# First mixer: multiplying four heads by a column each with four ScalarE activations instead of one VectorE instruction

## The chip, the cores and the metric

The kernel runs on one core of a Trainium2 chip. The metric is the device time of one execution in microseconds (us). The engines are called as in the profile: PE (TensorE: matmuls and transposes), PEld (its weight loads), DVE (VectorE), ACT (ScalarE), POOL (GpSimd) and SP (SyncE, which issues the large transfers).

## What is computed

The reference is a two-layer trunk over 256 positions of width 2048. Each layer is a modulated norm, a mixer, a gated residual, a second modulated norm, an MLP and a gated residual. The first layer's mixer runs eight gated DeltaNet heads and eight banded attention heads of 128 channels each beside one another. The parts that the change touches are the per-position factors in it:

```python
q = l2_norm(q.reshape(b_, t_, GDN_HEADS, GDN_DK)) * (GDN_DK ** -0.5)
k = l2_norm(k.reshape(b_, t_, GDN_HEADS, GDN_DK))
...
u = jnp.einsum('bhnij,bhnje->bhnie', tmat, vc * bc[..., None])
q_dec = qc * jnp.exp(gcum)[..., None]
...
o = rms_norm(o, norm_w) * jax.nn.silu(z.reshape(b_, t_, GDN_HEADS, GDN_DV).astype(f32))
...
qh = rms_norm(heads(q), q_norm_w).astype(f32) * (ATT_DH ** -0.5)
kh = rms_norm(heads(k), k_norm_w).astype(f32)
```

In each of these a matrix of 128 positions (the partitions) by 128 channels of one head is multiplied by one number per position.

## The kernel before

The weights stream from memory in pieces of 1 MB (`raw`). ACT casts each to a high part `wh` (L317), DVE takes the difference as a low part `wl` (L321), and PE multiplies both (L308); these products are in most of the program what PE does. Beside them the modulation vectors are reduced on DVE from pieces of the same size (`mraw`, L439, 2048 columns each), which share four buffers with the weight pieces, so SP can send the next transfer only when DVE has released a buffer.

The first mixer lies between about 240 and 560 us. It works in two groups of four heads (group 0 and group 1), and in tiles of 128 positions by four heads (128x512). The DeltaNet part prepares each tile in `gdn_tile`: squares of k and q (L1042, on ACT), an inverse square root by three Newton steps of tiny DVE instructions (L263 to L277), decay factors `gu` (L1046) and `gE`, then `gV` (v times a factor of k, L1069), then an inverse in six levels (L1100 to L1123: matmul, DVE mask into `gY`, matmul, DVE subtraction into `gX`, transposes, ACT copy into `gXt`). `gdn_group` then runs the chain over the tiles: `gvn` (L1147), the state `gS`, `gR` (L1160), `gqS` (L1165), the second `gvn` (L1171), the outputs `go` with their squares (L1185), an inverse root (`goy`), the multiplication of `go` (L1197), and transposes into a unit that the output projection reads. For the attention heads `att_qk` copies q or k out of PSUM (L1240), squares them (L1244), makes an inverse root (`ay`, L1247 and L271 to L276), multiplies (`aq`, L1250) and transposes (L1255 to L1257). It is called four times: q and k of group 0 near 250 us, q of group 1 near 363 us, k of group 1 near 427 us.

All of it is written as generators, whose steps are interleaved with the steps of the weight products. Each instruction has a priority from the order of emission, with the reductions of L439 put 20 later, and a list scheduler with a model of the durations sets the order on each engine. PE fills the time in these chains with products that are already loaded: `pg` from `wh` and `wl` in pieces of 512 columns, later of 256.

Of the kernel before, what the change touches and what calls it, by code (L numbers as in the profile page):

```python
# [13 lines left out]
AF = mybir.ActivationFunctionType  # L14
ALU = mybir.AluOpType
# [51 lines left out]
def wait(*tasks):  # L67
    for t in tasks:
        while not t.done:
            yield False  # L70
# [42 lines left out]
class Trunk:  # L113
# [212 lines left out]
    def split(self, src, hi, lo):  # L326
        for _ in self.split_steps(src, hi, lo):
            pass

    def bc(self, col, n=P):  # L330

        return col.unsqueeze(2).to_broadcast([P, col.shape[1], n])
# [691 lines left out]
    def gdn_tile(self, hg, t, kf, qf, vf, G):  # L1024
# [3 lines left out]
        nc = self.nc  # L1028
# [3 lines left out]
        for n, src in ((0, kf), (1, qf)):  # L1032
            ps = self.pm()
# [17 lines left out]
        nk = self.small(4, "gnk")  # L1051
        nc.vector.tensor_tensor(nk, v[:, :4], rn[:, :4], op=ALU.mult)
        be = self.small(4, "gbe")
# [5 lines left out]
        ps = self.pm()  # L1059
# [5 lines left out]
        ps = self.pm()  # L1065
        for h in range(4):
            self.tr(ps[:, h], vf[:, h, T])
        V = self.s2(tag="gV")
        nc.vector.tensor_tensor(V, ps, self.bc(nk), op=ALU.mult)  # L1069
        G["V", t] = V  # L1070
        yield

        ps = self.pm()
# [10 lines left out]
        ps = self.pm()  # L1084
# [6 lines left out]
        ps = self.pm()  # L1091
# [8 lines left out]
        for s in (2, 4, 8, 16, 32, 64):  # L1100
            nb = P // (2 * s)
            part = lambda a, n: a.rearrange("p h (b n c) -> p h b n c", n=2, c=s)[:, :, :, n]
            ps = self.pm()
# [6 lines left out]
            ps = self.pm()  # L1110
            if s < 64:
# [4 lines left out]
                ps = self.pm()  # L1116
# [10 lines left out]
    def gdn_group(self, hg, kc, qc, vc, gates):  # L1127

        nc = self.nc
        yield from wait(kc, qc, vc, gates)  # L1130
        yield
        kf, qf, vf = kc.result, qc.result, vc.result
        G = {}
        tiles = [Task(self.gdn_tile(hg, t, kf, qf, vf, G)) for t in range(2)]
        while not all(t.done for t in tiles):
            for t in tiles:
                if not t.done:
                    t.step()
            if all("X" + str(n) in G for n in range(2)):
                self.prep[hg].done = True  # L1140
            yield

        ps = self.pm()
        for h in range(4):
            self.mm(ps[:, h], G["Xt", 0][:, h], G["V", 0][:, h])
        v0 = self.s2(tag="gvn")
        nc.vector.tensor_tensor(v0, ps, self.bc(G["be", 0]), op=ALU.mult)  # L1147
        yield
        ps = self.pm()
        for h in range(4):  # L1150
            self.mm(ps[:, h], G["kd"][:, h], v0[:, h])
        S = self.s2(tag="gS")
        nc.scalar.copy(S, ps)
        yield
        ps = self.pm()
        for h in range(4):
            self.mm(ps[:, h], kf[:, h, P:], S[:, h])
        R = self.s2(tag="gR")
        for h in range(4):
            nc.vector.scalar_tensor_tensor(R[:, h], ps[:, h], self.neg_eg[:, hg * 4 + h : hg * 4 + h + 1], G["V", 1][:, h], op0=ALU.mult, op1=ALU.add)  # L1160
        qs = self.pm()
        for h in range(4):
            self.mm(qs[:, h], qf[:, h, P:], S[:, h])
        qS = self.s2(tag="gqS")
        nc.vector.tensor_tensor(qS, qs, self.bc(self.eg[:, hg * 4 : hg * 4 + 4]), op=ALU.mult)  # L1165
        yield
        ps = self.pm()
        for h in range(4):
            self.mm(ps[:, h], G["Xt", 1][:, h], R[:, h])
        v1 = self.s2(tag="gvn")  # L1170
        nc.vector.tensor_tensor(v1, ps, self.bc(G["be", 1]), op=ALU.mult)  # L1171
        ss = self.small(8, "goss")
        outs = []
        for t in range(2):
            yield
            ps = self.pm()
            for h in range(4):
                self.mm(ps[:, h], G["Pt", t][:, h], (v0, v1)[t][:, h])
            o = self.s2(tag="go")
            if t == 0:  # L1180
                nc.scalar.copy(o, ps)
            else:
                nc.vector.tensor_tensor(o, qS, ps, op=ALU.add)
            for h in range(4):
                nc.scalar.activation(ps[:, h], o[:, h], AF.Square, accum_out=ss[:, t * 4 + h : t * 4 + h + 1])  # L1185
            outs.append(o)
        yield
        r = self.small(8, "gor")
        for t in range(2):
            nc.vector.tensor_copy(r[:, t * 4 : t * 4 + 4], G["rq", t])  # L1190
        nc.vector.tensor_tensor(ss, ss, r, op=ALU.mult)
        nc.vector.tensor_tensor(ss, ss, r, op=ALU.mult)
        nc.vector.tensor_scalar(ss, ss, 1.0 / P, EPS, op0=ALU.mult, op1=ALU.add)
        rr = self.rsqrt(ss, 8, "go")
        nc.vector.tensor_tensor(rr, rr, r, op=ALU.mult)
        for t in range(2):
            nc.vector.tensor_tensor(outs[t], outs[t], self.bc(rr[:, t * 4 : t * 4 + 4]), op=ALU.mult)  # L1197
        yield

        res = qf  # L1200
        for t in range(2):
            ps = self.pm()
            for h in range(4):
                self.tr(ps[:, h], outs[t][:, h])
            nc.scalar.copy(res[:, :, t * P : t * P + P], ps)
            yield
        return res
# [24 lines left out]
    def att_qk(self, ps, nw, part=None):  # L1232

        nc = self.nc
        a, v = [], self.small(8, "ass")
        for t in range(2):
            x = self.s2(tag="aq")
            flat = x.rearrange("p h d -> p (h d)")
            if part is None:
                nc.scalar.copy(flat, ps[t])  # L1240
            else:
                nc.vector.tensor_tensor(flat, ps[t], part[:, t], op=ALU.add)
            for h in range(4):
                nc.scalar.activation(ps[t][:, h * P : h * P + P], x[:, h], AF.Square, accum_out=v[:, t * 4 + h : t * 4 + h + 1])  # L1244
            a.append(x)
            yield
        nc.vector.tensor_scalar(v, v, 1.0 / P, EPS, op0=ALU.mult, op1=ALU.add)  # L1247
        r = self.rsqrt(v, 8, "a")
        for t in range(2):
            nc.vector.tensor_tensor(a[t], a[t], self.bc(r[:, t * 4 : t * 4 + 4]), op=ALU.mult)  # L1250
        yield
        res = self.unit()
        for t in range(2):
            pt = self.pm()
            for h in range(4):  # L1255
                self.tr(pt[:, h], a[t][:, h])
            nc.scalar.activation(res[:, :, t * P : t * P + P], pt, AF.Copy, scale=nw)  # L1257
            if t == 0:
                yield
        return res  # L1260
# [551 lines left out]
```

## Time and profile before

| | |
|---|---|
| time, median of three runs | 2714.98 us (2714.04 to 2716.82) |
| time of the profiled execution | 2719.37 us |
| its span | 2717.6 us |
| mean granted clock of TensorE | 0.998 |
| PE, DVE, ACT busy | 2665.0, 2147.6, 1351.2 us |
| DVE, ACT busy in 240–260 us | 14.09, 17.59 of 20 |
| DVE, ACT busy in 340–360 us | 19.63, 14.34 of 20 |

A busy share is the mean over the whole span, and stages differ; so the stage of the mixer is read in windows. The chain of waits goes back from the last instruction to what released each; where PE carries it, PE never stood still. The rows that were read stand below.

### The profile page before, as it was taken

The page shows a single profiled execution, that of the slowest core. Times are in us where ns is not written, and L with a number is a line of the kernel's source. Part 1 is how long each engine was busy: PE and PEld are TensorE (multiplying, and loading weights), DVE is VectorE, ACT ScalarE, POOL GpSimd, SP SyncE. Part 2 cuts the span into 40 slices and gives each one's busy share as a digit, 9 for nine tenths or more (in the row PEclk, how much of TensorE's full clock was granted, in tenths as well). Part 3 has the DMA queues.
Part 4 walks back from the last instruction along what each step waited for, and adds up shares of the span by engine and source line. Part 5 has one row for each costly group of instructions (what it writes and reads, how often), then busy time and mean ns, then how long its engine had stood idle before and what let it go on. Part 6 is the DMA issues. An engine that isn't in the chain of part 4 may idle for free.

```text
span 2717.6 us, 39677 instructions
## 1 busy us (share of the span) xinstructions
PE 2665.0 (98%) x15664; PEld 2350.4 (86%) x15664; DVE 2147.6 (79%) x3081; ACT 1351.2 (50%) x1976; POOL 24.5 (1%) x98
## 2 busy tenths in 40 slices
PE   5999999999999999999999999999999999999999
PEld 5887989888888888888888888888888888888888
DVE  7998998987888888889889876897777855555554
ACT  3444454546445354454556544665555354454452
POOL 1000000000000000000000000000000000000000
PEclk9999999999999999999999999999999999999999
DMA  9986487867899898988456665554558855555554
GB/s 341 353 325 235 172 301 272 294 241 282 322 339 328 328 336 330 333 331 307 165 185 217 217 234 200 203 185 172 196 177 293 324 201 188 188 191 193 186 192 134
DMA packets 100459, 680.06 MB, mean 250 GB/s; under 512 B 11185, under 2 KB 14513, under 8 KB 19377
## 3 DMA queue, kind: packets, MB, share of 16 engines
q1 hardware_dynamic: 95376, 669.07, 68.5%
q10 hardware_dynamic: 4896, 8.46, 1.0%
q8 instruction: 123, 2.02, 0.3%
q14 instruction: 64, 0.52, 0.1%
HBM read 675.33 MB, written 2.16 MB: 249 GB/s over the span
## 4 chain that ended last, share of the span: by engine, by line
PE 90%; DVE 6%; DMA 1%; ACT 1%; issue 1%; SPq 0%; ACTq 0%; DVEq 0%
PE pw L308 70%; PE pg L308 13%; PE pm L311 4%; PE pm L308 3%; DVE mraw L439 2%; DVE wl L321 1%; PE pm L314 1%; DMA mraw<-in_mod_dram 1%; DVE u L1592 0%; ACT wh L317 0%; DVE hf L862 0%; ACT pm L1042 0%; DMA raw<-in_w_ab_dram 0%; DMA x<-in_x_dram 0%; DVE u L865 0%
## 5 line engine op out<-in xcount | busy, mean ns | idle before, releaser
L317 ACT CAST wh<-raw 128x1024 fp32r<-128x1024 f32 x870 | 907.1, 1051 | 1031.6 <-PE pw L308 732.9
L321 DVE TENSOR_TENSOR wl<-raw,wh 128x1024 fp32r<-128x1024 f32 x870 | 1048.7, 1220 | 463.8 <-ACT wh L317 349.6
L308 PE MATMUL pw<-u,wh 128*128 128x512 f32 x5584 | 1321.6, 391 | 2.6 <-DVE pad L973 1.9
L308 PEld LDWEIGHTS pw<-u,wh 128*128 128x128 f32 x5584 | 1032.2, 188 | 208.2 <-issue 3.3
L308 PEld LDWEIGHTS pw<-u,wl 128*128 128x128 f32 x5584 | 702.3, 191 | 21.3 <-issue 2.1
L308 PE MATMUL pw<-u,wl 128*128 128x256 f32 x5584 | 714.5, 283 | 0.3 <-DVE wl L321 0.3
L439 DVE SCALAR_TENSOR_TENSOR mraw<-mraw,crow 128x2048 f32<-128x2048 f32 x192 | 438.0, 2283 | 17.8 <-DMA mraw<-in_mod_dram 17.5
L308 PE MATMUL pg<-wh,u 128*128 128x512 f32 x864 | 281.6, 397 | 0.0
L308 PEld LDWEIGHTS pg<-wh,u 128*128 128x128 f32 x864 | 161.9, 188 | 32.1 <-issue 0.5
L925 DVE SCALAR_TENSOR_TENSOR x<-pw,mod,x 128x256 f32<-128x256 f32 x352 | 161.1, 478 | 22.6 <-PE pw L308 20.3
L308 PE MATMUL pg<-wl,u 128*128 128x512 f32 x432 | 169.9, 393 | 0.7 <-DVE wl L321 0.5
L308 PE MATMUL pg<-u,wh 128*128 128x256 f32 x672 | 124.6, 285 | 0.0
L308 PEld LDWEIGHTS pg<-u,wh 128*128 128x128 f32 x672 | 105.7, 192 | 0.3
L308 PEld LDWEIGHTS pg<-wl,u 128*128 128x128 f32 x432 | 81.4, 188 | 17.6 <-DVE wl L321 2.1
L308 PE MATMUL pg<-u,wl 128*128 128x256 f32 x336 | 95.3, 284 | 0.0
L308 PE MATMUL pm<-u,wh 128*128 128x256 f32 (+1 forms) x304 | 64.6, 310 | 19.2 <-ACT wh L317 19.2
L308 PEld LDWEIGHTS pm<-u,wh 128*128 128x128 f32 x304 | 49.1, 198 | 20.3 <-ACT wh L317 20.0
L308 PEld LDWEIGHTS pg<-u,wl 128*128 128x128 f32 x336 | 64.4, 192 | 0.1
L984 DVE SCALAR_TENSOR_TENSOR u<-pad,cst,u 128x256 f32<-128x256 f32 x144 | 60.6, 477 | 3.3 <-ACT u L978 3.2
L864 ACT ACTIVATE u<-hf,mod 128x256 fp32r<-128x256 f32 x64 | 29.3, 502 | 53.0 <-DVE hf L862 53.0
L1504 ACT ACTIVATE rl<-rs 128x512 f32<-128x512 f32 x64 | 40.4, 632 | 18.9 <-DVE rs L1499 14.4
L308 PE MATMUL pm<-u,wl 128*128 128x256 f32 x176 | 46.1, 290 | 3.1 <-DVE wl L321 3.1
(299 smaller groups left out, 1580.5 us busy)
## 6 DMA issues: line engine op xcount, KB each, us to landing
raw<-in_w_dram SPq DMA_DIRECT2D x256, 1024.0 KB, 5.0
mraw<-in_mod_dram SPq DMA_DIRECT2D x192, 1024.0 KB, 6.0
raw<-in_w_ab_dram SPq DMA_DIRECT2D x56, 1024.0 KB, 5.7
raw<-in_w_ssd_dram SPq DMA_DIRECT2D x48, 1024.0 KB, 4.9
raw<-in_w_sz_dram SPq DMA_DIRECT2D x32, 1024.0 KB, 4.9
raw<-in_wo_ssd_dram SPq DMA_DIRECT2D x32, 1024.0 KB, 4.8
raw<-in_wo_ab_dram SPq DMA_DIRECT2D x16, 1024.0 KB, 5.2
sE<-sd_rowd ACTq DMA_DIRECT2D x32, 256.0 KB, 4.9
```

Source lines behind the costliest of these rows:

```text
L308: self.nc.tensor.matmul(o, a, b, start=start, stop=stop, skip_group_check=True)
L311: self.nc.tensor.matmul(o, lhsT, rhs, start=True, stop=True, skip_group_check=True)
L314: self.nc.tensor.transpose(o, a, self.ident[:k, :k])
L317: a = self.nc.scalar.copy(hi, src)
L321: b = self.nc.vector.tensor_tensor(lo, src, hi.bitcast(F32), op=ALU.subtract)
L439: x = nc.vector.scalar_tensor_tensor(raw, raw, 1.0, self.crow, op0=ALU.mult, op1=ALU.mult, accum_out=t[:, f : f + 1])
L864: nc.scalar.activation(hi, h[:, f], AF.Identity, bias=shift[:, col])
L925: nc.vector.scalar_tensor_tensor(x[:, 2 * b + f], ps[:, f, n], g[:, 2 * cb + f : 2 * cb + f + 1], x[:, 2 * b + f], op0=ALU.mult, op1=ALU.add)
L984: nc.vector.scalar_tensor_tensor(h, pad[:, f, 1 + q : 257 + q], w[:, q, j : j + 1], h, op0=ALU.mult, op1=ALU.add)
L1504: nc.scalar.activation(rl, lo, AF.Relu)
```

## The change

A helper `heads(out, src, col)` issues, for each of four heads, one ScalarE activation Copy with the column of that head as its scale. It replaces a VectorE multiplication of the whole 128x512 tile by the four columns, broadcast over 128 channels, at six lines: L1069 (`gV`, four times), L1147 (`gvn`, two), L1165 (`gqS`, two), L1171 (`gvn`, two), L1197 (`go`, four) and L1250 (`aq`, eight): 22 instructions, for which there are 88. The helper adds five lines, so every later line has a number five higher after, and all 88 stand under the helper's line 333.

```diff
+    def heads(self, out, src, col):
+
+        for h in range(4):
+            self.nc.scalar.activation(out[:, h], src[:, h], AF.Copy, scale=col[:, h : h + 1])
...
         V = self.s2(tag="gV")
-        nc.vector.tensor_tensor(V, ps, self.bc(nk), op=ALU.mult)
+        self.heads(V, ps, nk)
...
-        nc.vector.tensor_tensor(v0, ps, self.bc(G["be", 0]), op=ALU.mult)
+        self.heads(v0, ps, G["be", 0])
...
-        nc.vector.tensor_tensor(qS, qs, self.bc(self.eg[:, hg * 4 : hg * 4 + 4]), op=ALU.mult)
+        self.heads(qS, qs, self.eg[:, hg * 4 : hg * 4 + 4])
...
-        nc.vector.tensor_tensor(v1, ps, self.bc(G["be", 1]), op=ALU.mult)
+        self.heads(v1, ps, G["be", 1])
...
         for t in range(2):
-            nc.vector.tensor_tensor(outs[t], outs[t], self.bc(rr[:, t * 4 : t * 4 + 4]), op=ALU.mult)
+            self.heads(outs[t], outs[t], rr[:, t * 4 : t * 4 + 4])
...
         for t in range(2):
-            nc.vector.tensor_tensor(a[t], a[t], self.bc(r[:, t * 4 : t * 4 + 4]), op=ALU.mult)
+            self.heads(a[t], a[t], r[:, t * 4 : t * 4 + 4])
```

The order of the other instructions in the stage changes too, since the scheduler places them anew. Three places are shown. The first is DVE's queue around `gR` of group 0; `mraw` is a piece of the modulation. Before:

```order
L439 SCALAR_TENSOR_TENSOR mraw_3369,mod_125<-mraw_3369,crow 128x2048
L1147 TENSOR_TENSOR gvn_3142<-pm_3137,gbe_2408 128x512
L321 TENSOR_TENSOR wl_3166<-raw_3159,wh_3165 128x1024
L447 TENSOR_TENSOR mod_125<-mod_125,cst 128x4
L1160 SCALAR_TENSOR_TENSOR gR_3180<-pm_3175,gd_neg,gV_2470 128x128 x4
L1165 TENSOR_TENSOR gqS_3190<-pm_3185,gd_eg 128x512
L1171 TENSOR_TENSOR gvn_3197<-pm_3192,gbe_2435 128x512
```

After:

```order
L452 TENSOR_TENSOR mod_125<-mod_125,cst 128x4
L321 TENSOR_TENSOR wl_3187<-raw_3180,wh_3186 128x1024
L444 SCALAR_TENSOR_TENSOR mraw_3522,mod_125<-mraw_3522,crow 128x2048
L1165 SCALAR_TENSOR_TENSOR gR_3201<-pm_3196,gd_neg,gV_2479 128x128 x4
L444 SCALAR_TENSOR_TENSOR mraw_3551,mod_125<-mraw_3551,crow 128x2048
L1188 TENSOR_TENSOR go_3251<-gqS_3211,pm_3246 128x512
L1195 COPY gor_3264<-grq_2410 128x4
```

The multiplications into `gvn` and `gqS` are gone from DVE, and a reduction (L444 in the new numbers) stands directly ahead of `gR`.

The second is ACT's queue at the q of group 1, at the end of the squares (`gss`) and of the decay factors (`gu`). Before, where the rows of `aq` are on DVE:

```order
L1042 ACTIVATE pm_3360,gss_3328<-pm_3360 128x128
L1046 ACTIVATE gu_3394<-Umask,gd_g 128x128
L1046 ACTIVATE gu_3421<-Umask,gd_g 128x128 x4
L1257 ACTIVATE u_3466<-pm_3467,cst 128x4x128
L317 CAST wh_3682<-raw_3680 128x1024
L1062 ACTIVATE gE_3475<-pm_3473 128x512
```

After:

```order
L1047 ACTIVATE pm_3393,gss_3361<-pm_3393 128x128
L1051 ACTIVATE gu_3433<-Umask,gd_g 128x128
L1051 ACTIVATE gu_3460<-Umask,gd_g 128x128 x4
L317 CAST wh_3620<-raw_3614 128x1024
L333 ACTIVATE aq_3340<-aq_3340,ay_3411 128x128 x4
L333 ACTIVATE aq_3378<-aq_3378,ay_3411 128x128 x4
L1262 ACTIVATE u_3505<-pm_3506,cst 128x4x128
L1067 ACTIVATE gE_3514<-pm_3512 128x512
```

The eight activations into `aq` come behind the last `gu` and a cast, ahead of the copy of the transposes (`u`).

The third is PE's queue at the k of group 1, where `aq` is transposed. Before:

```order
L308 MATMUL pg_4205<-u_290,wl_4130 128x256
L308 MATMUL pg_4205<-u_290,wh_4129 128x256 x2
L308 MATMUL pg_4205<-u_290,wl_4130 128x256
L308 MATMUL pg_4205<-u_290,wh_4129 128x256
L314 MATMUL pm_3969<-ident,aq_3839 128x128 x4
L311 MATMUL pm_3975<-gXt_3530,gY_3934 128x128 x4
L311 MATMUL pm_3981<-gXt_3543,gY_3948 128x128 x4
L314 MATMUL pm_4002<-ident,aq_3880 128x128 x4
L311 MATMUL pm_4008<-gV_3496,gXt_3530 128x128 x4
```

After:

```order
L314 MATMUL pm_3974<-ident,gX_3635 128x128 x4
L311 MATMUL pm_3980<-gX_3635,gLt_3570 128x128 x4
L314 MATMUL pm_3988<-ident,gX_3642 128x128 x4
L311 MATMUL pm_3994<-gX_3642,gLt_3583 128x128 x4
L314 MATMUL pm_4020<-ident,aq_3884 128x128 x4
L311 MATMUL pm_4026<-gXt_3575,gY_3985 128x128 x4
L311 MATMUL pm_4032<-gXt_3588,gY_3999 128x128 x4
L314 MATMUL pm_4053<-ident,aq_3925 128x128 x4
L308 MATMUL pg_3856<-wh_4005,u_1245 128x512
```

The products that stood ahead of the transposes of `aq` are elsewhere; the last level's matmuls from `gX` and `gLt` precede them directly.

DVE's queue from the later Newton steps of that k's inverse root (`ay`, `at`) to the last level was, before:

```order
L439 SCALAR_TENSOR_TENSOR mraw_4319,mod_126<-mraw_4319,crow 128x2048
L274 TENSOR_TENSOR at_3909<-ay_3907 128x8
L1108 TENSOR_TENSOR gY_3934<-pm_3929,lev_271 128x4x64
L275 TENSOR_TENSOR at_3909<-at_3909,an_3908 128x8
L1108 TENSOR_TENSOR gY_3948<-pm_3943,lev_271 128x4x64
L276 SCALAR_TENSOR_TENSOR ay_3907<-at_3909,ay_3907 128x8
L274 TENSOR_TENSOR at_3909<-ay_3907 128x8
L275 TENSOR_TENSOR at_3909<-at_3909,an_3908 128x8
L276 SCALAR_TENSOR_TENSOR ay_3907<-at_3909,ay_3907 128x8
L1250 TENSOR_TENSOR aq_3839<-aq_3839,ay_3907 128x512
L1250 TENSOR_TENSOR aq_3880<-aq_3880,ay_3907 128x512
```

and is, after:

```order
L275 TENSOR_TENSOR at_3954<-at_3954,an_3953 128x8
L444 SCALAR_TENSOR_TENSOR mraw_4259,mod_126<-mraw_4259,crow 128x2048
L1119 TENSOR_TENSOR gX_3635<-gX_3635,pm_3931 128x8x32
L1119 TENSOR_TENSOR gX_3642<-gX_3642,pm_3937 128x8x32
L276 SCALAR_TENSOR_TENSOR ay_3952<-at_3954,ay_3952 128x8
L274 TENSOR_TENSOR at_3954<-ay_3952 128x8
L275 TENSOR_TENSOR at_3954<-at_3954,an_3953 128x8
L276 SCALAR_TENSOR_TENSOR ay_3952<-at_3954,ay_3952 128x8
L1113 TENSOR_TENSOR gY_3985<-pm_3980,lev_271 128x4x64
L1113 TENSOR_TENSOR gY_3999<-pm_3994,lev_271 128x4x64
L444 SCALAR_TENSOR_TENSOR mraw_4324,mod_127<-mraw_4324,crow 128x2048
```

The root's last steps are done ahead of the last level's `gY`, and a reduction follows these.

## Rows read from the trace of the kernel before

**Rows 1.** The page: busy time of the engines; the chain that ended last
```profile
PE 2665.0 (98%) x15664; PEld 2350.4 (86%) x15664; DVE 2147.6 (79%) x3081; ACT 1351.2 (50%) x1976; POOL 24.5 (1%) x98
...
PE 90%; DVE 6%; DMA 1%; ACT 1%; issue 1%; SPq 0%; ACTq 0%; DVEq 0%
```

**Rows 2.** Instructions by line: duration ns min/median/max, first and last start us
```profile
L1069 DVE TENSOR_TENSOR gV<-pm,gnk x4: 673/680/692, 258.6 to 381.7; 128x512 f32<-128x512 f32 x4
...
L1197 DVE TENSOR_TENSOR go<-go,goy x4: 682/688/691, 352.9 to 453.2; 128x512 f32<-128x512 f32 x4
...
L1250 DVE TENSOR_TENSOR aq<-aq,ay x8: 679/683/691, 248.7 to 427.7; 128x512 f32<-128x512 f32 x8
...
L1046 ACT ACTIVATE gu<-Umask,gd_g x16: 401/406/415, 246.7 to 364.8; 128x128 f32<-128x128 f32 x16
```

**Rows 3.** Windows: us, PE, PEld, DVE, ACT, POOL busy, PEclk, DMA share, GB/s
```profile
240.00:260.00 20.00, 19.42 (x101) 14.31 (x99) 14.09 (x59) 17.59 (x83) 0.53 (x1) 1.00 0.54 201
...
340.00:360.00 20.00, 20.00 (x100) 16.56 (x99) 19.63 (x33) 14.34 (x52) 0.53 (x1) 1.00 0.85 304
360.00:380.00 20.00, 19.21 (x102) 15.48 (x101) 18.51 (x59) 11.30 (x36) 2.10 (x4) 1.00 0.76 277
...
420.00:440.00 20.00, 17.98 (x143) 17.64 (x142) 14.16 (x28) 6.19 (x9) 0.31 (x1) 0.91 0.79 270
```

**Rows 4.** PE's waits over 240–600 us: total us, times, longest us
```profile
PE pm L314 <- DVE aq L1250: 2.8, 2, 2.0
PE pm L314 <- DVE go L1197: 0.5, 1, 0.5
...
PE pm L311 <- DVE gV L1069: 0.2, 1, 0.2
```

**Rows 5.** Timeline of PE: start us, us, engine, line, operation [idle before, releaser]
```profile
364.60 0.63 PE L314 MATMUL pm<-ident,aq 128*128 128x128 f32 x4 [0.79 <-DVE aq L1250]
365.07 1.88 PE L311 MATMUL pm<-gu,SUmask 128*128 128x512 f32 x4
...
419.33 1.06 PE L311 MATMUL pm<-gY,gXt 128*128 128x128 f32 x8
420.22 0.60 PE L314 MATMUL pm<-ident,gX 128*128 128x128 f32 x4
...
427.94 1.09 PE L314 MATMUL pm<-ident,aq 128*128 128x128 f32 x4 [2.02 <-DVE aq L1250]
428.82 3.12 PE L311 MATMUL pm<-gXt,gY 128*128 128x128 f32 x16
431.78 0.60 PE L314 MATMUL pm<-ident,aq 128*128 128x128 f32 x4
```

**Rows 6.** A window of 1 us behind the longest wait, columns as in rows 3
```profile
429.00:430.00 1.00, 1.00 (x7) 1.00 (x6) 0.53 (x1) 0.94 (x2) 0.00 (x0) 0.50 0.87 357
```

**Rows 7.** Timeline of ACT near the q of group 1
```profile
355.55 1.14 ACT L1039 ACTIVATE gkd<-pm,gd_eg 128x128 f32<-128x128 f32 x4
...
363.60 1.57 ACT L1046 ACTIVATE gu<-Umask,gd_g 128x128 f32<-128x128 f32 x5
...
365.85 1.04 ACT L317 CAST wh<-raw 128x1024 fp32r<-128x1024 f32 x1
```

**Rows 8.** Timeline of DVE: the reductions, gR and the two late multiplications
```profile
329.21 2.28 DVE L439 SCALAR_TENSOR_TENSOR mraw<-mraw,crow 128x2048 f32<-128x2048 f32 x1
...
335.25 1.13 DVE L1160 SCALAR_TENSOR_TENSOR gR<-pm,gd_neg,gV 128x128 f32<-128x128 f32 x4 [1.94 <-PE pm L311]
...
363.76 1.29 DVE L1250 TENSOR_TENSOR aq<-aq,ay 128x512 f32<-128x512 f32 x2
...
423.27 2.29 DVE L439 SCALAR_TENSOR_TENSOR mraw<-mraw,crow 128x2048 f32<-128x2048 f32 x1 [2.24 <-DMA mraw<-in_mod_dram]
...
427.10 1.29 DVE L1250 TENSOR_TENSOR aq<-aq,ay 128x512 f32<-128x512 f32 x2
```

**Rows 9.** Transfers issued in 320–345 us: KB each, median us from issue to landing
```profile
mraw<-in_mod_dram SPq DMA_DIRECT2D x4, 1024.0 KB, 4.9
```

## Prediction

> **What bounds the kernel now.** The busy times and the chain of waits come first. PE is busy 98% of 2717.6 us and carries 90% of the chain, DVE 6% [rows 1]. A change to DVE and ACT therefore only moves the time where PE stands still for one of the two. All 22 multiplications lie between 248.7 and 453.2 us, in the first mixer [rows 2], so the windows of that stretch come next: DVE is close to full (19.63 of 20 us in 340–360, 18.51 in the next), ACT has room (14.34 and 11.30 us there), and PE is complete but for the window 420–440, where it lacks 2.02 us and its granted clock is 0.91 [rows 3]. PE's waits over 240–600 us say on what: 2.8 us on the attention multiplication (L1250) in two waits of 2.0 and 0.8, 0.5 us on the output one (L1197), 0.2 us on V (L1069) [rows 4]. Together 3.5 us is all that PE stands directly behind the instructions that the change replaces.
>
> The long wait has a tail. PE is released at 427.94 and then does 20 matmuls of 128 columns until 431.78, 3.84 us; 8 of that pitch took 0.89 us just before (419.33 to 420.22), so 20 would have taken 2.2 us [rows 5]. The granted clock reads 0.50 there, the 1.2 GHz level [rows 6]. The tail is 3.84 − 2.2 = 1.6 us. So **at most 3.5 + 1.6 = 5.1 us** can be won directly, 0.19% of the time. The 15 us of DVE work that go are not worth 15 us, since PE was covered by other matmuls in nearly all of them.
>
> **The bare exchange.** Removed: 22 TENSOR_TENSORs of 128x512 (four, four and eight in the rows, and two each on L1147, L1165 and L1171 that read alike) at 0.67 to 0.69 us [rows 2], 22 × 0.685 = 15.1 us of DVE. Added: 88 ACTIVATEs of 128x128 with a scale per partition. That operation is in the trace: four reading PSUM take 1.14 us in a row, and five reading SBUF 1.57 us, about 0.29 us each [rows 7], with a single one lasting 0.406 us [rows 2]. So 88 × 0.285 = 25.1 us more on ACT (35.7 us if none overlapped). Four heads take 1.14 to 1.28 us where one instruction took 0.685: the first head is there 0.28 us sooner, the last 0.5 to 0.6 us later. PE's transposes go head by head, so a chain that is fed from an idle engine changes by some tenths either way. What matters is the queue that the new instructions stand in.
>
> The Trainium skill, in Perfetto Trace Analysis, section Optimizing Scalar/DVE Operations, says both that grouping into larger operations helps throughput on a saturated engine and that moving work from a saturated DVE to ScalarE, or breaking instructions up where they cause bubbles elsewhere, can let work finish sooner. The trace agrees with the first part [rows 2, 7]; the second would make this change a gain, and it is the first rival below.
>
> **What the new order does, place by place.** The scheduler fills DVE's free time with other things, above all the modulation reductions (L439, 2.28 us each), and puts ACT's new instructions between casts and squares.
>
> 1. *First attention and V multiplications, 248–330 us.* The one wait is 0.2 us [rows 4]. ACT is at 17.59 us of 20 in 240–260 [rows 3] and gets 16 instructions there, 4.6 us; PE has the hoisted matmuls of the stretch to go on with. Term −0.2, bounds −0.2 and +1.
>
> 2. *gR of the first DeltaNet group.* Before, gR waits for PE until 335.25, with nothing of length ahead of it [rows 8]. Now a reduction stands directly ahead of it in DVE's queue. Its transfer goes into one of the four shared buffers, which the previous reduction (329.21, 2.28 us [rows 8]) frees near 330.4 by then, since a 0.69 us multiplication and more ahead of it are gone; landing takes 4.9 us [rows 9], giving 335.3, and 2.28 us of reduction end at 337.6, 2.3 us after gR used to start. If the transfer is out earlier it costs nothing. Bounds 0 and +2.3; taken +1.0, near the middle, as the release isn't to be read closer.
>
> 3. *Output multiplications of the first group.* Eight heads on ACT behind a cast, and the reduction on DVE ahead of their factors; 8 × 0.285 = 2.3 us instead of 1.29, PE paced by the later heads: +0.5, bounds 0 and +1.
>
> 4. *First q multiplications of the second group (L1250 at 363.76).* Before, DVE does them as soon as the inverse root is there, while ACT goes on with squares and the mask scalings up to 363.60 + 1.57 = 365.17 and then a cast [rows 7, 8]. Now they stand on ACT behind all of these: 365.17, plus the cast's 1.04 us, gives 366.2, the first head 366.5, the fourth 367.4; PE's four transposes end near 367.6, where before they began at 364.60 and gave way to the next at 365.07 [rows 5, 7]. Three more 512-column matmuls are ahead of the transposes, about 0.7 us of useful work. That is a loss of 2.5 − 0.7 = 1.8 us in PE, up to 3.7 us if the eight output heads push the whole burst by another 2 us. A reduction of 2.28 us is now in the middle of the inverse root too, but ends before the burst does. Taken +2.5. PE would then be idle for over 2 us, and the nearest row, the 2.02 us wait, was followed by the clock at 0.50 and 1.6 us lost; the 0.79 us wait by none (1.00 over 360–380) [rows 3, 5]. So +1.6. Term +4.1, bounds −0.8 (the old wait gone) and +5.3.
>
> 5. *Six levels of the second group.* Between the levels PE has 40 wide matmuls now instead of 27 wide and 37 narrow ones; DVE has about the same list per level. +0.5, bounds 0 and +3 (a reduction that waits for its transfer, as for 2.24 us at 423.27 [rows 8]).
>
> 6. *k multiplications of the second group (427.10).* Before, they were late because DVE stood 2.24 us for a transfer and then did 2.29 us of reduction in the middle of the inverse root [rows 8]. Now the inverse root ends ahead of the last level, ACT has the heads ready before PE comes, and the wait goes with its tail: −2.0 − 1.6 = −3.6, bounds −3.6 and 0 (the reduction that now stands ahead of the gXt additions waits for its transfer instead).
>
> 7. *Output of the second group.* Fewer matmuls between squares and transposes than before, and eight heads on ACT behind two casts: +0.5, bounds −0.5 (its old wait) and +1.5. *Attention heads after it*, packed closer together: +0.5, bounds 0 and +2.
>
> **Sum:** −0.2 + 1.0 + 0.5 + 4.1 + 0.5 − 3.6 + 0.5 + 0.5 = **+3.3 us**. The profiled execution took 2719.37 us, its span 2717.6; the median of the three runs is 2714.98, 4.4 us under it. The sum is a difference made in the one execution, and I put it on the median: 2714.98 + 3.3 = 2718.3 us. All bounds at the low end give −5.1 (rounded to 2710), and at the high end +16.1, which would need each bad case at once; half of that, 2723, is where I see the bad cases end singly, and 2726 with two of them.
>
> **Rivals.**
> *Relief.* The waits go (3.5 us) with the slow clock behind the long one (1.6 us) and nothing new comes: 2714.98 − 5.1 = 2709.9. For it: DVE is the fullest engine of the stretch after PE, and each of the listed waits is on a replaced instruction. Against it: points 2 and 4, where the new queues hold PE. It decides if the burst on ACT ends before PE comes to the q transposes. This is the Trainium skill's second rule (Perfetto Trace Analysis, section Optimizing Scalar/DVE Operations), that of offloading a saturated DVE; the trace bears it out for the k multiplications only. To pass 5.4 us it needs a little from closer packing besides; with point 6 alone it gives 2714.98 − 3.6 = 2711.4.
>
> *ACT's queue holds PE (the slower side).* The place is point 4: ACT's burst of squares and scalings with eight output heads ahead of it holds the q heads 3.7 us, the clock falls, 5.3 us; the same kind of hold at the output of the second group adds 1.5 and the reduction ahead of gR 2.3: +9.1, and the gain at point 6 of 3.6 doesn't come since a transfer wait moves into its place. 2714.98 + 9.1 = 2724.1. It decides from a wait of 3 us at the q transposes. For it: eight heads plus a burst whose end stands in [rows 7]. Against: PE has matmuls to fill which the scheduler moves ahead.
>
> *Nothing moves.* The waits trade places, the stretch is as long as before because PE's own matmuls set it (98% busy): 2715 ± 3.
>
> That the change doesn't do what it says (the multiplications staying on DVE) the order of instructions excludes: ACT has 88 more and DVE 22 fewer.
>
> **How the numbers follow.** My forecast (waits that go and waits that come, +3.3) has 0.42, nothing moving 0.12, relief 0.25, ACT's queue 0.21. A measurement of this kernel can tell some 0.2%, 5.4 us, from no change, so the bounds are 2709.6 and 2720.4. Forecast and nothing-moves put 0.12 above the upper one and 0.03 under the lower one; ACT's queue lies above with 0.20; relief is split by the lower one, 0.14 of it below if the closer packing pays. That makes faster 0.17, within 0.2% 0.51, slower 0.32. The range 2708 to 2726 leaves out about 2 in 10: relief with more packing below, a full ACT queue with transfer waits above.
>
> **What would show it.** In the profile of the changed kernel: PE's waits over 240–600 us should no longer name the k multiplications near 427, and no granted clock of 0.50 after it (point 6); a wait of 2 to 4 us on the ACT multiplication near 365, with the clock low behind it (point 4); a wait of about 1 us on gR near 336 with a reduction just ahead of gR in DVE's queue (point 2). DVE busy should fall by 15 us and ACT's rise by 25 to 36 us. If ACT's total rises by more, the heads don't overlap. The prediction is wrong if PE waits in the six levels or on transfers by more than 3 us together, or if PE arrives at the q transposes so late that ACT's burst is over.

## The result and the profile after

| | before | after |
|---|---|---|
| time, median (12 executions each) | 2715.32 us | 2722.06 us |
| lowest to highest | 2712.30 to 2719.96 | 2718.90 to 2727.62 |
| the profiled execution, its span | 2719.37, 2717.6 | 2727.62, 2725.9 |
| DVE, ACT busy | 2147.6, 1351.2 | 2137.6, 1375.0 |

The ratio is 1.0026, with an interval of 1.0017 to 1.0035: the change makes the kernel some 7 us slower. The forecast was 3.3 us slower. The profiled execution of the kernel after is the slowest of its twelve, 5.6 us over the median, so a second one is read below before its waits are counted.

The page of the kernel after, busy times and chain, against [rows 1]:

```profile
PE 2666.2 (98%) x15664; PEld 2349.7 (86%) x15664; DVE 2137.6 (78%) x3059; ACT 1375.0 (50%) x2064; POOL 24.2 (1%) x98
...
PE 80%; DVE 1%; ACT 0%; issue 0%; DMA 0%; ACTq 0%; DVEq 0%
```

ACT has 88 more instructions and is busy 23.8 us longer, a little under the 25 to 36 that were forecast; DVE has 22 fewer and is busy 10 us less, where 15 were forecast, and where the other 5 went isn't traced here. (The shares of the chain add up to 81% here and to 99% before, so they can't be set against each other.) PE's work is the same 15664 matmuls. So the 7 us are waits, or work at a slower pace. PE's waits over 240–600 us of the kernel after (total us, times, longest us), against [rows 4]:

```profile
PE pm L314 <- DVE as L1301: 2.3, 1, 2.3
PE pg L308 <- ACT wh L317: 2.3, 1, 2.3
PE pw L308 <- DVE cvt L1220: 1.1, 1, 1.1
PE pm L311 <- ACT gu L1051: 1.0, 1, 1.0
PE pm L314 <- DVE gX L1119: 0.7, 2, 0.4
PE pm L311 <- ACT gV L333: 0.4, 1, 0.4
...
PE pm L314 <- ACT go L333: 0.2, 1, 0.2
PE pm L314 <- ACT aq L333: 0.2, 1, 0.2
```

The replaced multiplications are nearly gone from the list (0.4 on `gV`, 0.2 each on `go` and `aq`), as the relief theory wanted. In their place stand a cast, the mask factors `gu`, the levels' `gX`, and the normalization of the last attention head. Two windows with the largest of them, columns as in [rows 3]:

```profile
360.00:380.00 20.00, 17.70 (x100) 14.17 (x99) 19.07 (x65) 17.72 (x61) 2.03 (x4) 1.00 0.67 235
...
480.00:500.00 20.00, 17.66 (x121) 16.64 (x120) 13.46 (x17) 7.23 (x14) 0.00 (x0) 0.91 0.69 248
```

In 360–380 PE lacks 2.3 us and ACT is busy for 17.72 of 20 us, where it was 11.30 [rows 3]. The timeline of ACT there shows why; a cast that PE's next product needs stands behind the mask factors, and the heads of `aq` behind the cast:

```profile
364.74 1.58 ACT L1051 ACTIVATE gu<-Umask,gd_g 128x128 f32<-128x128 f32 x5
366.20 1.05 ACT L317 CAST wh<-raw 128x1024 fp32r<-128x1024 f32 x1
367.21 2.45 ACT L333 ACTIVATE aq<-aq,ay 128x128 f32<-128x128 f32 x8
```

Eight heads take 2.45 us, where two VectorE instructions took 1.29 [rows 8].

### The profile page after: what moved, and what is told of

It is laid out like the page before. It is cut to its first block, busy times and chain, and to the rows that moved or that the text cites. A ratio compares the mean times of both kernels' runs of the same rounds, so it can differ in the third digit from the quotient of the medians.

```text
span 2725.9 us, 39759 instructions
## 1 busy us (share of the span) xinstructions
PE 2666.2 (98%) x15664; PEld 2349.7 (86%) x15664; DVE 2137.6 (78%) x3059; ACT 1375.0 (50%) x2064; POOL 24.2 (1%) x98
## 3 DMA queue, kind: packets, MB, share of 16 engines
q8 instruction: 123, 2.02, 0.3%
## 4 chain that ended last, share of the span: by engine, by line
PE 80%; DVE 1%; ACT 0%; issue 0%; DMA 0%; ACTq 0%; DVEq 0%
PE pw L308 70%; PE pg L308 7%; PE pm L311 1%; PE pm L308 1%; PE pm L314 1%; DVE wl L321 0%; DMA sE<-sd_rowd 0%; ACT wh L317 0%; DVE hf L867 0%; ACT u L869 0%; DVE u L989 0%; DVE x L930 0%; DVE rst L275 0%; DVE rst L274 0%; ACT sE L1403 0%
## 5 line engine op out<-in xcount | busy, mean ns | idle before, releaser
L444 DVE SCALAR_TENSOR_TENSOR mraw<-mraw,crow 128x2048 f32<-128x2048 f32 x192 | 438.8, 2287 | 21.4 <-DMA mraw<-in_mod_dram 21.3
```

The lines of the kernel that those rows point to most:

```text
L444: x = nc.vector.scalar_tensor_tensor(raw, raw, 1.0, self.crow, op0=ALU.mult, op1=ALU.mult, accum_out=t[:, f : f + 1])
```

## The experiments

The scheduler re-ordered the whole stage, so two things came at once: the exchange of instructions, and a new order. To take them apart, most of the kernels below carry a written order: a list that names, for each engine, all instructions by their place in the code, and ties neighbours together by an order-only dependency. The edit is then the list alone, or the list and a few lines. That the list costs nothing by itself is borne out below, by a kernel that carries one and came out at a ratio of 1.0000.

### Exchange and order, each alone

First, the code of the kernel after with every other instruction in the order of the kernel before, each four heads in ACT's list where the multiplication was in the whole (`_pin` ties the instructions to the list):

```diff
 trunk(tc, ins, out)
+_pin(tc)
```

> The 88 activations on ACT, and every other instruction of each engine in the order of the kernel before; each group of four heads stands in ACT's queue where the VectorE multiplication stood in the scheduler's list. Theory O (the new order costs, above all the modulation reductions that were pulled ahead of waiting instructions on DVE): the exchange alone is nearly free, 2713 to 2717 us against 2715.3 before and 2722.1 after. Rival A (the activations themselves cost, as ACT's queue holds what PE waits for): 2720 to 2724 us, with PE waiting for casts or gu behind the heads as in the kernel after.

Measured: 2722.36 us, ratio to before 1.0031 (1.0021 to 1.0041). The exchange alone, 6.8 us over before, costs as much as the whole change. My theory O fell with this. Second, the code of the kernel before in the order of the kernel after, the multiplications put into DVE's list; the edit is the same line with another list.

> The VectorE multiplications of before, and every other instruction of each engine in the order of the kernel after; the multiplications of aq and go stand right behind the last step of their roots. Theory O (the order costs): 2719 to 2724 us, with the wait of 2.3 us on the last attention head and its slow clock. Rival A (the activations cost): 2713 to 2717 us, since ACT is relieved of all 88. DVE has 15 us more in this kernel than the order was made for, so a further loss of 1 to 3 us would not speak against O.

Measured: 2733.35 us, 1.0057 (1.0044 to 1.0070), five executions between 2727.06 and 2733.60. Neither theory had it in its range. The order of after is made for a DVE that has 15 us less to do, and with the multiplications on DVE it is worse than either kernel. This doesn't measure the order's own cost, which stays open.

In the first of the two, PE's order is that of the kernel before, instruction for instruction, so each start can be set against the other's. PE's timeline of that kernel:

```profile
250.14 1.21 PE L314 MATMUL pm<-ident,aq 128*128 128x128 f32 x4
251.87 1.21 PE L314 MATMUL pm<-ident,aq 128*128 128x128 f32 x4 [0.53 <-ACT aq L333]
...
368.68 1.20 PE L314 MATMUL pm<-ident,aq 128*128 128x128 f32 x4 [0.39 <-ACT aq L333]
...
372.18 1.12 PE L311 MATMUL pm<-gu,SUmask 128*128 128x512 f32 x2 [1.21 <-ACT gu L1051]
```

Four transposes take 1.20 us, where they took 0.63 [rows 5]. They do not wait long for any one head, so only 0.39 us is listed as a wait, but each of them waits for the next head, and the heads come every 0.29 us, where PE takes 0.11 for a transpose. And `gu` comes 1.21 us late, as the heads stand ahead of it on ACT. That is **pacing**, a loss that the list of waits doesn't show. Set against a second execution of the kernel before (below), PE falls back by 2.7 us at q and k of group 0 with `gu` (from −1.7 to +1.0), 0.5 at `gV`, 1.0 at `go`, 2.4 at q and `gu` of group 1 (2.07 to 4.52), 0.5 at `gV`, 0.5 at k, 1.1 at `go`; some of it is won back in between, and by 472 us it is 7.5 us in all.

### The parts of the exchange, in the old order

The same with a part of the 22 multiplications at a time:

```diff
-nc.vector.tensor_tensor(a[t], a[t], self.bc(r[:, t * 4 : t * 4 + 4]), op=ALU.mult)
+self.heads(a[t], a[t], r[:, t * 4 : t * 4 + 4])
...
+_pin(tc)
```

> The order of the kernel before on every engine; of the 22 multiplications only the eight into aq are 32 activations, each group in its place. Theory P (PE is paced by heads that come every 0.29 us, and gu waits behind them in ACT's queue): from the rows of the kernel with all 88 in this order, 2.7 us at group 0, 2.5 at q and 0.3 at k of group 1: +5.5 us, 2721 us (2719 to 2722.5). Rival E (every moved multiplication costs alike, 6.8 us / 22 each): +2.5 us, 2718 us.

Measured: 2720.82 us, 1.0017 (1.0008 to 1.0026), 4.5 us over the before of the same chip (2716.31).

> As the last, but only the four into gV and the four into go are activations. Theory P: 0.55 and 0.57 us at gV, 1.06 and 1.1 us at go: +3.3 us, 2719 us (2717.5 to 2720.5). Rival E: +2.5 us, 2718 us.

Measured: 2720.11 us, 1.0017 (1.0008 to 1.0025), 3.8 us over.

> As the last, but only the four into gvn and the two into gqS are activations. Theory P: no row of PE moved at these places, so no cost: 2715.5 us (2714 to 2717). Rival E: +1.9 us, 2717.5 us.

Measured: 2716.21 us, 1.0000 (0.9991 to 1.0009). The three parts give 4.5 + 3.8 − 0.1 = 8.2 us, against 6.8 for all of them at once, with some 2.5 us of uncertainty on each. All three lie in the ranges of theory P; the second cost half a microsecond more than its rows. Rival E, the same cost for each, wants 2.5, 2.5 and 1.9 us, and with that uncertainty the times alone exclude it in none of the three. PE's rows speak against it: at the places of `gvn` and `gqS` they did not move by over 0.3 us, and E has no reason for that.

### The pace, made slower, and kept on DVE

If the pace is the cause, more and smaller activations must cost more:

```diff
-self.nc.scalar.activation(out[:, h], src[:, h], AF.Copy, scale=col[:, h : h + 1])
+for c in (slice(0, 64), slice(64, 128)):
+    self.nc.scalar.activation(out[:, h, c], src[:, h, c], AF.Copy, scale=col[:, h : h + 1])
```

> The order of the kernel before; the eight into aq are 64 activations of 64 columns each, two for a head, which doubles the number of instructions that pace PE and not the work. Theory P (PE is paced by ACT's instructions): a half head will take 0.15 to 0.29 us more or less, say 0.24, four heads 1.9 us instead of 1.2; 0.7 us more for each of the two tiles of group 0, for q's first and k's first, and as much again where gu waits behind: +3 to +5 us over the kernel with 32 activations (2720.8 us), 2724 us (2722.5 to 2727). Rival W (what costs is that the operand lies on ACT, whatever the pace): 2721 us.

Measured: 2726.70 us, 1.0045 (1.0033 to 1.0058), 12.2 us over before, where the 32 whole heads cost 4.5. The columns are the same, the count of instructions is double. The instruction (duration ns), and PE's timeline at group 0, with a window of 1 us behind it:

```profile
L334 ACT ACTIVATE aq<-aq,ay x64: 331/333/353, 249.0 to 439.7; 128x64 f32<-128x64 f32 x64
```

```profile
249.69 1.76 PE L314 MATMUL pm<-ident,aq 128*128 128x128 f32 x4
252.16 0.80 PE L314 MATMUL pm<-ident,aq 128*128 128x128 f32 x2 [0.72 <-ACT aq L334]
253.11 0.95 PE L314 MATMUL pm<-ident,aq 128*128 128x128 f32 x2
253.85 1.92 PE L314 MATMUL pm<-ident,u 128*128 128x128 f32 x8
```

```profile
254.00:255.00 1.00, 1.00 (x7) 1.00 (x6) 0.00 (x0) 1.00 (x5) 0.00 (x0) 0.50 0.00 0
...
377.00:378.00 1.00, 1.00 (x7) 1.00 (x6) 1.00 (x3) 0.77 (x1) 0.00 (x0) 0.50 0.06 16
```

A half head lasts 0.333 us, and the two of one head are done every 0.48 us: PE's pairs of transposes at 252.16 and 253.11 begin 0.95 us apart. Here even the granted clock falls to 0.50 behind the thinly spaced transposes, so that the next eight, at 253.85, take 1.92 us instead of 1.04. It reads 0.50 once more from 374 to 379 us, behind a wait of 1.9 us on `gu`. Rival W, for which only the move counts, falls: the move is the same, the loss is over twice as large. Theory P had the direction and the place, but not the clock, and came out 2.7 us low. The two slow stretches, some 3 and 7 us long at half speed, can have cost up to 5 us (an estimate), and the 32 whole heads had none there; so the 7.7 us that the half heads cost beyond the whole ones are not the pace alone.

The reverse is to make the split without the move:

```diff
-nc.vector.tensor_tensor(a[t], a[t], self.bc(r[:, t * 4 : t * 4 + 4]), op=ALU.mult)
+for h in range(4):
+    nc.vector.tensor_scalar(a[t][:, h], a[t][:, h], r[:, t * 4 + h : t * 4 + h + 1], None, op0=ALU.mult)
...
+_pin(tc)
```

> The order of the kernel before; the eight into aq stay on DVE, as four instructions of 128 columns each (32 for 8), so that the split is made but not the move. Theory P with ACT's queue: DVE's heads come some 0.2 us apart and nothing stands longer in ACT's queue, so gu isn't late: +0 to +1.5 us, 2716 to 2717.5 us. Rival S (the split itself costs, as much as on ACT): 2720 to 2722 us.

Measured: 2716.61 us, 1.0007 (0.9998 to 1.0016), 2.2 us over the before of the same chip (2714.46), not to be told from no change. Rival S falls. PE's timeline at group 0:

```profile
249.76 1.04 PE L314 MATMUL pm<-ident,aq 128*128 128x128 f32 x8
250.64 1.04 PE L314 MATMUL pm<-ident,u 128*128 128x128 f32 x8
```

Eight transposes go through in 0.88 us, at full pace: DVE has done enough heads by the time PE comes, and no activation stands ahead of `gu`. So neither the split nor the number of instructions on an engine costs anything that can be told; what costs is that ACT, which is slower at it, is also the engine with the squares and the mask factors. No kernel changes one of these two and leaves the other, the slower pace and the fuller queue: how the loss divides between them is read from the rows.

### The largest waits of the kernel after, one by one

Three edits of the written orders. In the first, four modulation reductions of the kernel after stand behind what they were ahead of on DVE: the output factors of group 0, the root of q of group 1 (two), the normalization of the last attention head.

```diff
-L444 SCALAR_TENSOR_TENSOR mraw_3788,mod_127<-mraw_3788,crow 128x2048
...
-L444 SCALAR_TENSOR_TENSOR mraw_3843,mod_126<-mraw_3843,crow 128x2048
...
+L444 SCALAR_TENSOR_TENSOR mraw_3788,mod_127<-mraw_3788,crow 128x2048
+L444 SCALAR_TENSOR_TENSOR mraw_3843,mod_126<-mraw_3843,crow 128x2048
```

> The kernel after, word for word in its order, but for four of its modulation reductions on DVE: one behind the output factors of group 0 instead of ahead of them, two behind the root of q of group 1 instead of ahead of it and in its middle, one behind the normalization of the last attention head instead of ahead of it. Theory O: the wait of 2.3 us at 367 goes for the most part (2.0), that of 2.3 us at 491 with its slow clock as well (2.3 + 1.7 = 4.0): 2722.1 - 6.0 = 2716 us, 2714.5 to 2718. Rival A: ACT's burst holds the cast and the heads as before, and at most the last wait goes: 2718 to 2722 us.

Measured: 2727.41 us, 1.0041 (1.0029 to 1.0054), above both ranges, and by its median slower still than the kernel after, though the two intervals overlap. PE's waits, and DVE ahead of the low part:

```profile
PE pg L308 <- ACT wh L317: 2.3, 1, 2.3
PE pg L308 <- DVE wl L321: 2.1, 1, 2.1
PE pm L311 <- ACT gV L333: 2.0, 2, 1.6
```

```profile
377.79 2.29 DVE L444 SCALAR_TENSOR_TENSOR mraw<-mraw,crow 128x2048 f32<-128x2048 f32 x1 [1.91 <-DMA mraw<-in_mod_dram]
```

The wait on the cast is untouched, although the root of q was now early: ACT's queue alone holds it. And the reductions, put behind the root of q, stand ahead of the root of k's norm, and hold `gV` through it. They also give their buffers back later: SP issues the next two modulation transfers at 370.63, where it did at 366.30 in the kernel after, the next reduction waits 1.91 us for its transfer, and the low part behind it holds PE for 2.1 us. The wait at the last attention head was gone, but that it went for this reason isn't shown, as the second execution of the kernel after, below, lacks it too.

In the second, the cast on which PE waits stands ahead of the burst on ACT.

```diff
+L317 CAST wh_3620<-raw_3614 128x1024
...
-L317 CAST wh_3620<-raw_3614 128x1024
```

> The kernel after in its own order, but for one cast on ACT, that on which PE waits 2.3 us near 367 in both profiled executions: it stands ahead of the burst of squares and mask factors instead of behind it. Theory Q (ACT's queue is full there, with as much work ahead of PE's next operands whatever its order): the wait on the cast goes, PE does its matmuls 2.3 us earlier and then waits for the heads of aq, which come at the same time as before: a gain of about 1.1 us, 2721 us, and a new wait of 1 to 1.5 us on aq. Rival C (the cast's place alone is at fault): the whole wait goes, a gain of 2.3 us or, where the clock fell behind it, 3.5 us: 2718.5 to 2720 us, and no new wait.

Measured: 2722.47 us, 1.0028 (1.0019 to 1.0038): nothing won. Rival C falls. PE's timeline, and those of ACT and DVE:

```profile
368.97 0.33 PE L314 MATMUL pm<-ident,aq 128*128 128x128 f32 x1 [3.38 <-ACT aq L333]
```

```profile
368.51 2.46 ACT L333 ACTIVATE aq<-aq,ay 128x128 f32<-128x128 f32 x8 [0.84 <-DVE ay L276]
```

```profile
365.28 2.28 DVE L444 SCALAR_TENSOR_TENSOR mraw<-mraw,crow 128x2048 f32<-128x2048 f32 x1
...
368.31 0.17 DVE L276 SCALAR_TENSOR_TENSOR ay<-at,ay 128x8 f32<-128x8 f32 x1
```

The wait is now 3.38 us long and on the heads. ACT itself waits 0.84 us for the root, which has a reduction of 2.28 us in its middle. Theory Q gave the new wait, but at less than half its length, since I had left the root out. Two chains, ACT's burst and DVE's root with its reduction, end within a microsecond of each other here; to shorten one of them, as in each of these two kernels, gives nothing.

The third is the kernel before, with the reduction that waited for its transfer at 423.27 [rows 8] put behind the multiplications of k:

```diff
-L439 SCALAR_TENSOR_TENSOR mraw_4319,mod_126<-mraw_4319,crow 128x2048
...
 L1250 TENSOR_TENSOR aq_3880<-aq_3880,ay_3907 128x512
+L439 SCALAR_TENSOR_TENSOR mraw_4319,mod_126<-mraw_4319,crow 128x2048
```

> The kernel before in its own order, but for one reduction on DVE, that which waits 2.24 us for its transfer at 423.27: it stands behind the two multiplications of k of group 1. Theory O: the wait of 2.0 us at 427 goes with its 1.6 us of slow clock: 2715.3 - 3.6 = 2711.7 us, 2711 to 2713. Rival: the transfer's wait only comes back at the next reduction or in gXt, 2715 us.

Measured: 2716.36 us, 1.0002 (0.9993 to 1.0011): nothing, and yet PE's wait at 427 was gone from its trace. Part of it came back in another place, on a copy by ACT:

```profile
429.11 1.13 PE L311 MATMUL pm<-gV,gXt 128*128 128x128 f32 x8 [0.83 <-ACT u L1257]
```

The interval, −1.9 to +3.0 us, excludes a gain of 3.6 us. That asked whether the wait belongs to the kernel at all.

### Both kernels again

> The kernel before, unchanged: a second profiled execution. Theory V: the wait of 2.0 us at 427 with 1.6 us of slow clock behind it hangs on when one transfer landed in the first profiled execution (2719.4 us, 4 us over the median), and is gone or under 0.5 us here, with a span of 2712 to 2715 us. Rival: it belongs to the kernel, and stands here again with 1.5 to 2.5 us.

Measured: 2718.01 us, a span of 2716.2. At the k of group 1 PE's timeline, the reduction on DVE, and a window there, are now:

```profile
427.65 0.28 PE L308 MATMUL pg<-u,wh 128*128 128x256 f32 x1
427.77 0.60 PE L314 MATMUL pm<-ident,aq 128*128 128x128 f32 x4
428.20 1.95 PE L311 MATMUL pm<-gXt,gY 128*128 128x128 f32 x16
```

```profile
422.96 2.28 DVE L439 SCALAR_TENSOR_TENSOR mraw<-mraw,crow 128x2048 f32<-128x2048 f32 x1
```

```profile
429.00:430.00 1.00, 1.00 (x12) 1.00 (x11) 0.91 (x3) 1.00 (x3) 0.00 (x0) 1.00 1.04 442
```

No wait, no slow clock, and 16 matmuls in 1.95 instead of 3.12 us [rows 5, 6]. DVE came to the reduction 2 us later than in the first execution and did not wait for its transfer. The span is over the one that I expected, as this execution was 1.8 us later by 235 us, ahead of the mixer. Between 235 us and the transposes of `rsy` behind the mixer (590.10 in the first, 589.18 in this) it took 352.1 us, the first 354.8: the 2.0 us wait and its 1.6 us tail cost that execution at most 2.7 us in the stage.

The wait comes and goes from execution to execution; it is no accident of the first alone. Of the five profiled executions in which DVE does these multiplications in the old order, two have it, the first and that of the kernel with only `gvn` and `gqS` on ACT:

```profile
423.64 2.29 DVE L444 SCALAR_TENSOR_TENSOR mraw<-mraw,crow 128x2048 f32<-128x2048 f32 x1 [2.28 <-DMA mraw<-in_mod_dram]
```

PE waited 2.08 us behind it, without a slow clock (last section), and this execution took 2716.44 us, where the median of its kernel is 2716.21. So the wait by itself doesn't lift an execution over the median, and what made up the 4.4 us of the first isn't shown.

> The kernel after, unchanged: a second profiled execution. Waits that come from ACT's queue stand again: 1.0 us on gu near 256, 2.3 us on a cast near 367. Theory V: the wait of 2.3 us on the last attention head near 491, which hangs on a transfer, differs here by over 1 us, or the slow clock behind it is missing, and the span is 2718 to 2722 us. Rival: all is the same, and the span is over 2723 us.

Measured: 2721.51 us, a span of 2719.8. Its waits on PE:

```profile
PE pg L308 <- ACT wh L317: 2.3, 1, 2.3
PE pw L308 <- DVE cvt L1220: 1.1, 1, 1.1
PE pm L311 <- ACT gu L1051: 1.0, 1, 1.0
PE pm L308 <- POOL u L1282: 1.0, 1, 1.0
```

The cast, `cvt` and `gu` stand again with the same lengths; the wait on the last attention head is gone. In the first execution DVE had a transfer to wait for ahead of that head:

```profile
488.86 2.29 DVE L444 SCALAR_TENSOR_TENSOR mraw<-mraw,crow 128x2048 f32<-128x2048 f32 x1 [2.36 <-DMA mraw<-in_mod_dram]
```

So the former three belong to the kernel, the latter to the transfers of one execution. From PE's matmul on `gd_g` near 242 us to the transposes of `rsy` the stage took 348.2 and 345.5 us in the two executions of before and 354.9 and 352.5 in those of after: the 7 us arise inside the mixer.

## Why the prediction was right in its direction and short in its size

The way it goes was right, and the time lies in the range; the size was half of what was measured, 3.3 against some 6.7 us. The step that failed is **point 6**, the −3.6 us at the k multiplications. Its mechanism came: in both executions of after the root ends early and PE doesn't wait at k. But it took a wait with its slow clock from one profiled execution as a property of the kernel, and put it on the median. The kernel before without this wait gained nothing (1.0002, 0.9993 to 1.0011), and a second execution of before doesn't have it. The sign for this was in [rows 8]: what released DVE there was a transfer. Without this term the sum is +6.9 us. That this meets the measured value is partly luck, as the other terms show:

- Point 1 (−0.2 predicted, bounds −0.2 and +1): +1.05 at `gu`, since the eight heads of q, 2.44 us on ACT, and in the new order more squares than before stand ahead of the mask factors; with +0.2 each at `aq` and `gV` over the bound. The matmuls that I named as cover were used up before `gu` came.
- Point 2 (+1.0): nothing for PE. The hold itself came: the reduction ahead of `gR` waited 0.69 us for its transfer, and `gR` began at 336.90, directly behind it, where before it had stood waiting for PE and begun at 335.25 [rows 8]. PE had products to do until 337.37 and did not wait; the term left this cover out.

```profile
334.68 2.29 DVE L444 SCALAR_TENSOR_TENSOR mraw<-mraw,crow 128x2048 f32<-128x2048 f32 x1 [0.69 <-DMA mraw<-in_mod_dram]
...
336.90 1.12 DVE L1165 SCALAR_TENSOR_TENSOR gR<-pm,gd_neg,gV 128x128 f32<-128x128 f32 x4
```

```profile
337.37 0.93 PE L311 MATMUL pm<-gR,gXt 128*128 128x128 f32 x6
```

- Point 3 (+0.5): no wait that the list shows; the scheduler had put single matmuls between the transposes of `go`.
- Point 4 (+4.1, the largest): the place is right, and the cause, ACT's burst with the heads and a cast. But PE waited on the cast, ahead of the heads. The length was 2.29 us in both executions against 0.79 before, +1.5 us, not +2.5; the slow clock that I added came in the second execution and not in the first.
- Point 5 (+0.5): waits of 0.33 and 0.41 us on `gX` and 0.27 on `gXt` in the first execution, 0.27 on `gXt` alone in the second.
- Point 7 (+1.0 with attention): 0.2 us at `go`; 2.3 us with a slow clock at the last attention head in the first execution, none in the second; and 0.9 us more on `cvt` in both, which I had not seen. With point 5 that is over 3 us in the levels and on transfers, the prediction's own sign of being wrong, in the first execution and not in the second.

The prediction's reading that PE is complete but for 420–440 us also leaves out 0.58 and 0.79 us, which [rows 3] show in 240–260 and 360–380.

The sentence of the bare exchange that the change of pace is worth "some tenths either way" was the second error. In the old order it costs 0.6 us for four transposes (1.20 against 0.63), at each place where PE comes straight at the heads, and `gu` pays again for standing behind them. The free scheduler of the kernel after covers part of this with matmuls between the transposes, and pays elsewhere. Both ways cost about 7 us; that the amounts are so near may be chance, and where each microsecond of the kernel after lies isn't settled.

Of the rivals, relief is refuted: the replaced instructions' waits went, and others came. So is the one in which nothing moves (2715 ± 3). The Trainium skill (Perfetto Trace Analysis, section Optimizing Scalar/DVE Operations) says that with a saturated DVE moving work to ScalarE may make sense; here it did not, as DVE got 10 us free and the kernel lost 7. The rival with ACT's queue named the right mechanism, and its 2724.1 us lies nearer to the measured time than my 2718.3. Its price, with a hold of 3.7 us at q, was too high, and its claim that a transfer wait would replace the gain at point 6 was needless, since there was no gain to replace.

## What to carry to other kernels

Before a wait in one profiled execution is counted as a gain, look whether what released it, or the engine ahead of it, was a transfer; a second profile shows which waits stay, and one that is missing there can still come again in a third. An operation that is split into pieces on a slower engine sets the pace of whoever consumes the pieces, and a consumer that waits a little at each piece doesn't appear in a list of waits: compare its instructions' pitch instead. Moving work to the engine with the lower busy share is no relief if that engine has its bursts exactly where the work lands.

## What was not expected of the hardware

How long PE stands idle didn't by itself decide whether its clock fell. Behind waits of 2.02 us in the first execution of before, and 2.29 us in the second of after, it read 0.50; behind the same wait of 2.29 us in the first of after it read 1.00, and so it did behind one of 2.1 us in the kernel with only `gvn` and `gqS` on ACT, whose wait and windows are:

```profile
PE pm L314 <- DVE aq L1255: 2.9, 2, 2.1
```

```profile
427.00:428.00 1.00, 0.00 (x0) 0.00 (x0) 0.90 (x4) 0.00 (x0) 0.00 (x0) 1.00 0.67 229
...
429.00:430.00 1.00, 1.00 (x11) 1.00 (x10) 1.00 (x2) 1.00 (x2) 0.00 (x0) 1.00 0.92 377
```

With half heads it fell behind a listed wait of only 0.72 us, where PE's transposes had come one every 0.48 us. And the length of an activation hardly follows its columns here: 0.333 us for the 64 columns of a half head, and 0.387 for the 128 of a head in the kernel with all 88 in the old order.
